# Decode attention of a hybrid layer: scores of both paged branches first, outputs afterwards

## The chip, the cores and the metric

The kernel runs on one core of a Trainium2 chip. The metric is the device time of one execution in microseconds (us), taken as the median of several runs. Besides, one execution is profiled, which gives the span of the core and a trace of every engine: PE (TensorE matmuls), PEld (its weight loads), DVE (VectorE), ACT (ScalarE), POOL (GpSimd) and SP (which here only issues transfers).

## What is computed

One inference step of a one-layer decoder, for a prompt of 1024 tokens and for 8 sampling sequences with one new token each:

```
p = rmsnorm(x, norm_g) @ w_in            # 1032 tokens x 2840 columns
q, cmp_kv, slc_kv, win_kv, gate logits, za, u, zp = split(p)
o_attn  = gate0*compressed(q) + gate1*selected(q) + gate2*window(q)   # 8 query heads, 2 KV heads, dim 64
o_pool  = causal means of u over 2/4/8/16 tokens, minus u, times pool_w and pool_scale
y = rmsnorm(x + concat(o_attn*silu(za), o_pool*silu(zp)) @ w_out, final_g)
```

For the 8 sampling sequences ("decode") each branch has a past of 256 tokens: the selected branch reads two pages of 128 rows per sequence from `cache_slc_kv` through a page table, the window branch reads 256 rows from `cache_win_kv`, and the compressed branch uses 15 blocks that an earlier stage of the kernel has computed. With so few blocks all of the past is selected, so the selected branch is plain attention over 257 keys (256 old ones and the new one), and so is the window branch.

## The kernel before, in words

The work stands in this order in the code: projection columns in token-major form (keys, values, gates), the compression of blocks together with the projection of the queries (`feat_unit`, lines 404 to 406), `decode()`, the pooling group, then the attention of the prompt in 32 units (`stage1` scores and softmax, `stage2` transposition and output), and between the steps of those units the filler work (the `za` gates with lines 979 to 981, the output projection with line 1053).

A scheduler orders the instructions of each engine ahead of time. It goes by a priority, mostly the place in the code, by estimated durations and by free buffers. `decode()` is emitted with a raised priority, as are the steps of the attention units. Thus in the machine code the decode instructions are strewn between the `feat_unit` matmuls of the pooling group (columns U and ZP, four groups `g`), which come after it in the code. Each engine then runs its own list strictly in order, and waits where an operand or a buffer isn't ready.

Names that matter below:

- `kvx` (4 buffers of 128 x 512 f32): a page of the selected branch, or 256 rows of the window of one sequence, keys and values together. It is fetched by an indirect transfer (line 640) or a plain one (line 644), both issued from POOL's queue.
- `dkt` (line 646): transposed keys in a PSUM bank of the ring `S` (3 banks). `kxh` and `kxl` (lines 656 and 657): their high and low part, one buffer each for four sequences.
- `vx` (8 buffers): the values split in a high part (ACT, line 651) and a low part (POOL, line 652). All eight sequences of a branch are held until the output matmuls of that branch (`dO`, line 684) have read them.
- `qx` and `px`: block-diagonal queries and probabilities, zeroed on POOL (lines 555 and 557). `pd`: the scores of a branch, and then its probabilities. `od`, `oq`: the sum of the outputs.
- PSUM rings: `S` with 3 banks (decode, and later the scores of the prompt), `tp` with 3 banks (`ps_t`: transpositions, and in the pooling group `ut`, line 810, and `yp`, line 849), `O` and `pj` with one bank each.
- The memory of `decode()`'s pool `dp` is given to the pool `at` of the prompt's attention (`qt`, `Ps`, `Pw`) when `decode()` is closed, each buffer as its last reader in `dp` is done. `stage1` of the first unit stands in the code within group 3 of the pooling part.
- `load_tile` (lines 393 and 143/144) fetches the weights of a `feat_unit` through SP and splits them on ACT and DVE.

`decode()` goes through the compressed branch first (lines 608 to 620), and then through the two other branches one after the other: scores, softmax, output.

Of the kernel before, what the change touches and what calls it, by code (L numbers as in the profile page):

```python
# [7 lines left out]
F32 = mybir.dt.float32  # L8
F32R = mybir.dt.float32r
I32 = mybir.dt.int32  # L10
BF16 = mybir.dt.bfloat16
AF = mybir.ActivationFunctionType
# [6 lines left out]
NB = 8  # L19
# [17 lines left out]
def r32(ap):  # L37
    return ap.bitcast(F32)
# [3 lines left out]
def hybrid_step_kernel(ctx, tc, xp, xs, ccmp, cslc, cwin, spool, ptab, norm_g, w_in, cmp_pe, cmp_w1,  # L42
                       cmp_w2, pool_w, pool_scale, w_out, final_g,
                       y_p, y_s, ncmp_p, nslc_p, nwin_p, npool_p, ncmp_s, nslc_s, nwin_s, npool_s):
    nc = tc.nc
# [11 lines left out]
    def ps_s(name="S"):  # L57
        return psum.tile([128, 512], F32, name=name, tag="S", bufs=3)

    def ps_t(name="tp"):  # L60
        return psum.tile([128, 512], F32, name=name, tag="tp", bufs=3)
# [22 lines left out]
    ident = pers.tile([128, 128], F32, name="ident")  # L84
# [254 lines left out]
    for br in range(2):  # L339
# [7 lines left out]
        for t in range(9):  # L347
            p, n = tok_unit(hi, lo, cn, t)
            if t < 8:
                f = kvf_tile(t)  # L350
# [11 lines left out]
                if t % 4 == 3:  # L362
                    c0 = (KS, KW)[br] + (t - 3) * 128
# [4 lines left out]
            else:  # L368
                f = p
# [76 lines left out]
    p = ps_t("pe_ps")  # L446
# [9 lines left out]
    Kcs = keep.tile([128, 128], F32, name="Kcs")  # L456
    Vcs = keep.tile([128, 128], F32, name="Vcs")
    zh = cp.tile([128, 8, NCOL + 4], F32R, name="zh")
    zl = cp.tile([128, 8, NCOL + 4], F32R, name="zl")
    for kind in range(2):  # L460
# [8 lines left out]
        for grp in range(3):  # L469
            tiles = pair_tiles(grp)  # L470
            for par in range(2):
                p = ps_t("z_ps")
                for m in range(4):
                    c0 = par * 256 + kind * 128
# [8 lines left out]
        for j in range(2):  # L483
            hi, lo = load_tile(dap(cmp_w1, (kind * 2 + j) * 16 * 64 * 128,
                                   [[128, 128], [16384, 8], [1, 128]]), cp)
            for s in range(8):
                mv = zh[:, s, j:j + NCOL + 2]
                first, last = j == 0 and s == 0, j == 1 and s == 7
# [3 lines left out]
                                 start=False, stop=last)  # L492
# [7 lines left out]
        if kind == 0:  # L500
            p = ps_t("kc_ps")
# [8 lines left out]
        else:  # L510
            p = ps_t("vc_ps")
            for kv in range(2):
                nc.tensor.matmul(p[:64, kv * 64:(kv + 1) * 64], H[:, kv * 192:kv * 192 + 64], w2v,
                                 start=True, stop=True)
# [4 lines left out]
            p = ps_t("vcs_ps")  # L519
            for kv in range(2):  # L520
                nc.tensor.matmul(p[:, kv * 64:(kv + 1) * 64], H[:, kv * 192 + 64:kv * 192 + 192], w2v,
                                 start=True, stop=True)
# [5 lines left out]
    for pt in range(4):  # L528
        hi, lo = load_tile(w_cols(C_Q + pt * 128))
        for c in range(3):  # L530
            p, t0, n = feat_unit(hi, lo, c)
# [16 lines left out]
    def decode():  # L548

        dp = des.enter_context(tc.tile_pool(name="dp", bufs=1, reuse_waits="tile"))  # L550

        qs = dp.tile([128, NB, 8], F32, name="qs")
# [1 line left out]
        nc.vector.memset(qs, 0.0)  # L554
        nc.gpsimd.memset(r32(qx), 0.0)
        px = dp.tile([128, 2, NB, 2, 64], F32R, name="px")
        nc.gpsimd.memset(r32(px), 0.0)

        def diag(ap):

# [10 lines left out]
        Kcs = dp.tile([128, 128], F32, name="Kcs")  # L571
# [26 lines left out]
        Pd = [Pd[0], Pd[1], Pd[0]]  # L598

        def dsoft(br, src, n):  # L600
            mx, nm, sm, rc = (st[:, br, k:k + 1] for k in range(4))
            nc.vector.tensor_reduce(mx, src, axis=AX.X, op=OP.max)
            nc.vector.tensor_scalar(nm, mx, -1.0, None, op0=OP.mult)
            nc.scalar.activation(Pd[br][:, :n], src, AF.Exp, bias=nm, accum_out=sm)
            nc.vector.reciprocal(rc, sm)
            nc.vector.tensor_scalar(Pd[br][:, :n], Pd[br][:, :n], rc, g64[:, br:br + 1], op0=OP.mult, op1=OP.mult)

        p = ps_s("dsc")
        nc.tensor.matmul(p[:64, :128], qs.rearrange("p b h -> p (b h)"), Kcs, start=True, stop=True)
        scs = Pd[0][:, :128]  # L610
        nc.vector.tensor_add(scs, p[:64, :128], cmask.rearrange("p b c -> p (b c)"))
        dsoft(0, scs, 128)
        p = ps_s("dpt")
        nc.tensor.transpose(p[:, :64], Pd[0][:, :128], ident[:64, :64])
        PcT = dp.tile([128, 64], F32, name="PcT")
        nc.vector.tensor_copy(PcT, p[:, :64])
        od = dp.tile([64, 128], F32, name="od")
        p = ps_s("dO0")
        nc.tensor.matmul(p[:64, :128], PcT, Vcs, start=True, stop=True)
        nc.vector.tensor_copy(od, p[:64, :128])  # L620
        for br in range(2):
            vx = []
            kn = dp.tile([128, NB], F32, name="kn", bufs=2)
            p = ps_s("dkn")
            nc.tensor.transpose(p[:, :NB], knew[br][:, :128], ident[:NB, :NB])
            nc.vector.tensor_copy(kn, p[:, :NB])
            sp = ps_s("dS")
            for b in range(0, NB, 2):
                if b % 4 == 0:
                    KXh = dp.tile([128, 4, 258], F32R, name="kxh")  # L630
                    KXl = dp.tile([128, 4, 258], F32R, name="kxl")
                    nc.vector.memset(r32(KXh[:, :, 257]), 0.0)
                    nc.vector.memset(r32(KXl[:, :, 257]), 0.0)
                    nc.vector.tensor_copy(KXh[:, :, 256], kn[:, b:b + 4])
                    nc.vector.tensor_sub(KXl[:, :, 256], kn[:, b:b + 4], r32(KXh[:, :, 256]))
                p = ps_s("dkt")
                for bb in range(2):
                    f = dp.tile([128, 512], F32, name="kvx", bufs=4)
                    if br == 0:
                        nc.gpsimd.indirect_dma_start(out=f, out_offset=None, in_=cslc,  # L640
                                                     in_offset=bass.IndirectOffsetOnAxis(
                                                         ap=idx[:, b + bb:b + bb + 1], axis=0))
                    else:
                        nc.gpsimd.dma_start(f, cwin[b + bb].rearrange("(p two) c -> p (two c)", two=2))
                    for par in range(2):
                        nc.tensor.transpose(p[:, (bb * 2 + par) * 128:(bb * 2 + par + 1) * 128],
                                            f[:, par * 256:par * 256 + 128], ident)

                    v = dp.tile([128, 2, 2, 128], F32R, name="vx", bufs=8)
                    fv = f.rearrange("p (two f c) -> p two f c", two=2, f=2)[:, :, 1]  # L650
                    nc.scalar.activation(v[:, :, 0], fv, AF.Copy)
                    nc.gpsimd.tensor_sub(v[:, :, 1], fv, r32(v[:, :, 0]))
                    vx.append(v)
                src = p.rearrange("p (b k) -> p b k", b=2)
                sl = (slice(None), slice(b % 4, b % 4 + 2), slice(0, 256))
                nc.scalar.activation(KXh[sl], src, AF.Copy)
                nc.vector.tensor_sub(KXl[sl], src, r32(KXh[sl]))
                for bb in range(b, b + 2):
                    w = qx[:, bb].rearrange("p f c -> p (f c)")
                    nc.tensor.matmul(sp[:, :258], w, KXh[:, bb % 4], start=bb == 0, stop=False)  # L660
                    nc.tensor.matmul(sp[:, :258], w, KXl[:, bb % 4], start=False, stop=bb == NB - 1)
            ss = Pd[br + 1]
            nc.scalar.activation(ss[:, :257], sp[64:, :257], AF.Copy)
            nc.vector.tensor_add(ss[:, :257], sp[:64, :257], ss[:, :257])
            dsoft(br + 1, ss[:, :257], 257)
            P_ = Pd[br + 1]
            dd = dp.tile([64, NB], F32, name="dd", bufs=2)
            nc.vector.tensor_scalar(dd, bmask, P_[:, 256:257], None, op0=OP.mult)
            p = ps_s("dptr")
            for par in range(2):  # L670
                nc.tensor.transpose(p[:, par * 64:(par + 1) * 64], P_[:, par * 128:(par + 1) * 128],
                                    ident[:64, :64])
            nc.tensor.transpose(p[:NB, 128:192], dd, ident[:64, :64])
            for par in range(2):
                src = p[:, par * 64:(par + 1) * 64].rearrange("p (b h) -> p b h", b=NB)
                ph, pl = (diag(px[:, par, 0, part, :]) for part in range(2))
                nc.scalar.activation(ph, src, AF.Copy)
                nc.vector.tensor_sub(pl, src, r32(ph))
            E_ = dp.tile([NB, 64], F32, name="dE", bufs=2)
            nc.vector.tensor_copy(E_, p[:NB, 128:192])  # L680
            p = ps_s("dO")
            for b in range(NB):
                for par in range(2):
                    nc.tensor.matmul(p[:, :256], px[:, par, b].rearrange("p f c -> p (f c)"), vx[b][:, par].rearrange("p f c -> p (f c)"),
                                     start=b == 0 and par == 0, stop=b == NB - 1 and par == 1)
            oq = dp.tile([64, 128], F32, name="oq")
            nc.scalar.activation(oq, p[64:, :128], AF.Copy)
            nc.vector.tensor_add(od, od, p[:64, :128])
            nc.vector.tensor_add(oq, oq, p[:64, 128:256])
            nc.vector.tensor_add(od, od, oq)  # L690
            p = ps_s("dOn")
            nc.tensor.matmul(p[:64, :128], E_, knew[br][:, 128:256], start=True, stop=True)
            nc.vector.tensor_add(od, od, p[:64, :128])
        p = ps_s("dOt")
        nc.tensor.transpose(p[:, :64], od, ident[:64, :64])
        odv = p[:, :64].rearrange("p (b h) -> p h b", h=8)
# [585 lines left out]
```

## Time and profile before

| | us |
|---|---|
| median of 3 runs | 638.68 (638.59 to 640.15) |
| the profiled execution, its own time | 638.69 |
| its span | 637.0 |
| PE busy in the span | 622.3 (98%) |
| DVE busy | 423.4 (66%) |
| ACT busy | 367.3 (58%) |
| POOL busy | 270.7 (43%) |

The busy time of an engine is the union of its instructions; matmuls overlap each other, and their ends are modelled. The time of an execution is the span and 1.7 us around it. Stretches are given in us from the span's start: the decode work lies between about 186 and 284, within the pooling group's matmuls, and the prompt's attention after it.

### The profile page before, as it was taken

The page shows a single profiled execution, that of the slowest core. Times are in us where ns is not written, and L with a number is a line of the kernel's source. Part 1 is how long each engine was busy: PE and PEld are TensorE (multiplying, and loading weights), DVE is VectorE, ACT ScalarE, POOL GpSimd, SP SyncE. Part 2 cuts the span into 40 slices and gives each one's busy share as a digit, 9 for nine tenths or more (in the row PEclk, how much of TensorE's full clock was granted, in tenths as well). Part 3 has the DMA queues.
Part 4 walks back from the last instruction along what each step waited for, and adds up shares of the span by engine and source line. Part 5 has one row for each costly group of instructions (what it writes and reads, how often), then busy time and mean ns, then how long its engine had stood idle before and what let it go on. Part 6 is the DMA issues. An engine that isn't in the chain of part 4 may idle for free.

```text
span 637.0 us, 12211 instructions
## 1 busy us (share of the span) xinstructions
PE 622.3 (98%) x4160; PEld 578.5 (91%) x4160; DVE 423.4 (66%) x1253; ACT 367.3 (58%) x947; POOL 270.7 (43%) x412
## 2 busy tenths in 40 slices
PE   8999999999999999999999999999999999999995
PEld 5999999999999899999899899789999988898895
DVE  6754234637364647466887999778978787877653
ACT  5654233526223333217887988777877777776652
POOL 6144004314035615005556767645554556444510
PEclk9999999999999999999999999999999999999999
DMA  8436106956224433333313357313113030101101
GB/s 281 152 90 157 34 1 201 314 196 181 74 79 133 138 102 95 92 110 101 100 35 99 100 182 214 107 30 101 37 50 100 18 100 16 67 19 67 51 2 66
DMA packets 63742, 65.13 MB, mean 102 GB/s; under 512 B 4488, under 2 KB 55120, under 8 KB 63640
## 3 DMA queue, kind: packets, MB, share of 16 engines
q1 hardware_dynamic: 53631, 44.55, 23.4%
q0 software_dynamic: 4000, 12.76, 6.2%
q10 hardware_dynamic: 6048, 7.05, 3.2%
q8 instruction: 33, 0.54, 0.4%
q14 instruction: 30, 0.24, 0.1%
HBM read 50.98 MB, written 15.68 MB: 105 GB/s over the span
## 4 chain that ended last, share of the span: by engine, by line
PE 93%; DVE 2%; ACT 1%; issue 1%; DMA 1%; POOL 1%; DVEq 0%; POOLq 0%; ACTq 0%
PE pj L1053 14%; PE S L777 10%; PE tp L902 9%; PE pa L404 7%; PE pa L406 7%; PE pa L405 7%; PE O L920 5%; PE O L919 5%; PE pa L277 4%; PE pa L275 3%; PE pa L276 3%; PE pj L979 2%; PE pj L980 2%; PE pj L981 2%; PE xtp_ps L230 1%; PE pj L1057 1%
## 5 line engine op out<-in xcount | busy, mean ns | idle before, releaser
L908 DVE TENSOR_TENSOR pl<-tp,ph 128x512 fp32r<-128x512 f32 (+1 forms) x136 | 89.9, 670 | 22.7 <-ACT ph L907 22.0
L777 PE MATMUL S<-KT,qt 128*128 128x320 f32 (+10 forms) x400 | 98.2, 346 | 3.0 <-DVE sm L736 3.0
L907 ACT ACTIVATE ph<-tp 128x512 fp32r<-128x512 f32 (+1 forms) x136 | 78.0, 580 | 38.3 <-PE tp L902 28.7
L404 PE MATMUL pa<-x,ws_hi 128*128 128x384 f32 (+1 forms) x288 | 93.7, 325 | 0.0
L406 PE MATMUL pa<-x,ws_lo 128*128 128x384 f32 (+1 forms) x288 | 92.9, 323 | 0.0
L405 PE MATMUL pa<-x,ws_hi 128*128 128x384 f32 (+1 forms) x288 | 92.7, 322 | 0.0
L1053 PE MATMUL pj<-wo,mh 128*128 128x512 f32 (+1 forms) x272 | 84.1, 387 | 0.0
L920 PE MATMUL O<-pl,V 128*128 128x256 f32 x264 | 75.7, 305 | 0.2
L919 PE MATMUL O<-ph,V 128*128 128x256 f32 x264 | 74.0, 296 | 0.0
L777 PEld LDWEIGHTS S<-KT,qt 128*128 128x128 f32 x400 | 63.7, 189 | 9.0 <-DVE sm L736 3.0
L796 POOL TENSOR_SCALAR Ps<-Ps,sm,gates 128x64 f32<-128x64 f32 (+5 forms) x88 | 62.9, 722 | 19.9 <-DVE sm L792 7.3
L789 ACT ACTIVATE Ps<-Ps,sm 128x64 f32<-128x64 f32 (+4 forms) x96 | 60.2, 628 | 16.4 <-DVE sm L736 14.8
L404 PEld LDWEIGHTS pa<-x,ws_hi 128*128 128x128 f32 x288 | 54.2, 188 | 0.5
L405 PEld LDWEIGHTS pa<-x,ws_hi 128*128 128x128 f32 x288 | 54.2, 188 | 0.4 <-issue 0.3
L406 PEld LDWEIGHTS pa<-x,ws_lo 128*128 128x128 f32 x288 | 54.2, 188 | 0.2
L277 PE MATMUL pa<-w_hi,x 128*128 128x256 f32 (+1 forms) x184 | 52.9, 288 | 1.2 <-DVE x L236 1.2
L275 PE MATMUL pa<-w_hi,x 128*128 128x256 f32 (+1 forms) x184 | 53.6, 292 | 0.0
L1053 PEld LDWEIGHTS pj<-wo,mh 128*128 128x128 f32 x272 | 47.2, 188 | 6.1 <-ACT mh L1205 0.3
L920 PEld LDWEIGHTS O<-pl,V 128*128 128x128 f32 x264 | 49.8, 189 | 3.1 <-DVE pl L908 0.6
L276 PE MATMUL pa<-w_lo,x 128*128 128x256 f32 (+1 forms) x184 | 52.4, 285 | 0.0
L1053 PE MATMUL pj<-wo,ml 128*128 128x512 f32 (+1 forms) x136 | 52.1, 383 | 0.0
L919 PEld LDWEIGHTS O<-ph,V 128*128 128x128 f32 x264 | 49.9, 189 | 1.8
(302 smaller groups left out, 1556.1 us busy)
## 6 DMA issues: line engine op xcount, KB each, us to landing
ws_raw<-in_w_in SPq DMA_DIRECT2D x32, 256.0 KB, 3.1
qt<-q_d SPq DMA_DIRECT2D x64, 128.0 KB, 2.9
x_t<-in_x_prompt SPq DMA_DIRECT2D x8, 512.0 KB
wo_raw<-in_w_out SPq DMA_DIRECT2D x8, 512.0 KB, 4.3
r<-in_x_prompt SPq DMA_DIRECT2D x8, 512.0 KB, 3.1
out<-r SPq DMA_DIRECT2D x7, 512.0 KB, 3.1
q_d<-qhl ACTq DMA_DIRECT2D x8, 384.0 KB, 4.0
out<-kvf ACTq DMA_DIRECT2D x5, 512.0 KB, 3.1
```

The costliest lines, as they stand in the source:

```text
L275: nc.tensor.matmul(p[:n, :cn], xh[c][:, k, ts_], hi[:, k, :cn], start=k == 0, stop=False)
L276: nc.tensor.matmul(p[:n, :cn], xh[c][:, k, ts_], lo[:, k, :cn], start=False, stop=False)
L277: nc.tensor.matmul(p[:n, :cn], xl[c][:, k, ts_], hi[:, k, :cn], start=False, stop=k == 7)
L404: nc.tensor.matmul(p[:, :n], hi[:, k, :], xh[c][:, k, :], start=k == 0, stop=False)
L405: nc.tensor.matmul(p[:, :n], hi[:, k, :], xl[c][:, k, :], start=False, stop=False)
L406: nc.tensor.matmul(p[:, :n], lo[:, k, :], xh[c][:, k, :], start=False, stop=k == 7)
L777: nc.tensor.matmul(S[:, :ln], qt[:, f, h, :], KT[:, kv, k0 + a:k0 + a + ln], start=f == 0, stop=f == 1)
L907: nc.scalar.activation(ph[:, :m], tp[:, :m], AF.Copy)
L908: nc.vector.tensor_sub(pl[:, :m], tp[:, :m], r32(ph[:, :m]))
L919: nc.tensor.matmul(O[:, :256], vv, ph[:, a * 256:(a + 1) * 256], start=False, stop=False)
L920: nc.tensor.matmul(O[:, :256], vv, pl[:, a * 256:(a + 1) * 256], start=False, stop=last)
L1053: nc.tensor.matmul(p, a[:, k % 4, :], w, start=first and kk == 0, stop=last and kk == 2)
```

## The change

The three branches are put in another order. `dscores(br)` holds the score part of a paged branch, `dout(br, ...)` its output part. The order in the code becomes: scores of the selected branch; zeros for `px`; scores of the window branch; output of the selected branch; the window's values; the whole compressed branch; output of the window branch. In the window branch the keys of two sequences share one `kvx` buffer and come in transfers of their own, 16 transfers of half the size in all in place of 8, and the values come in the other half of these. The transposed keys `dkt` go to the `tp` ring. The compressed branch keeps its probabilities in a buffer of the name `oq`. The first output that is added to `od` is now that of the selected branch.

```
-        nc.gpsimd.memset(r32(px), 0.0)
...
-        p = ps_s("dsc")
-        nc.tensor.matmul(p[:64, :128], qs.rearrange("p b h -> p (b h)"), Kcs, start=True, stop=True)
-        scs = Pd[0][:, :128]
-        nc.vector.tensor_add(scs, p[:64, :128], cmask.rearrange("p b c -> p (b c)"))
-        dsoft(0, scs, 128)
...
-        nc.vector.tensor_copy(od, p[:64, :128])
-        for br in range(2):
+        def split_v(v, fv):
+            nc.scalar.activation(v[:, :, 0], fv, AF.Copy)
+            nc.gpsimd.tensor_sub(v[:, :, 1], fv, r32(v[:, :, 0]))
+
+        def dscores(br):
...
-                p = ps_s("dkt")
+                p = ps_t("dkt")
+                if br == 1:
+                    f = dp.tile([128, 512], F32, name="kvx", bufs=4)
+                    for bb in range(2):
+                        nc.gpsimd.dma_start(f[:, bb * 256:(bb + 1) * 256].rearrange("p (two c) -> p two c", two=2),
+                                            cwin[b + bb].rearrange("(p two) c -> p two c", two=2)[:, :, :128])
                 for bb in range(2):
-                    f = dp.tile([128, 512], F32, name="kvx", bufs=4)
                     if br == 0:
+                        f = dp.tile([128, 512], F32, name="kvx", bufs=4)
                         nc.gpsimd.indirect_dma_start(out=f, out_offset=None, in_=cslc,
...
-                    else:
-                        nc.gpsimd.dma_start(f, cwin[b + bb].rearrange("(p two) c -> p (two c)", two=2))
...
-                    v = dp.tile([128, 2, 2, 128], F32R, name="vx", bufs=8)
-                    fv = f.rearrange("p (two f c) -> p two f c", two=2, f=2)[:, :, 1]
-                    nc.scalar.activation(v[:, :, 0], fv, AF.Copy)
-                    nc.gpsimd.tensor_sub(v[:, :, 1], fv, r32(v[:, :, 0]))
-                    vx.append(v)
+                    if br == 0:
+                        v = dp.tile([128, 2, 2, 128], F32R, name="vx", bufs=8)
+                        split_v(v, f.rearrange("p (two f c) -> p two f c", two=2, f=2)[:, :, 1])
+                        vx.append(v)
...
+        def win_values():
+            vx = []
+            for b in range(0, NB, 2):
+                f = dp.tile([128, 512], F32, name="kvx", bufs=4)
+                for bb in range(2):
+                    fv = f[:, bb * 256:(bb + 1) * 256].rearrange("p (two c) -> p two c", two=2)
+                    nc.gpsimd.dma_start(fv, cwin[b + bb].rearrange("(p two) c -> p two c", two=2)[:, :, 128:])
+                    v = dp.tile([128, 2, 2, 128], F32R, name="vx", bufs=8)
+                    split_v(v, fv)
+                    vx.append(v)
+            return vx
+
+        def dout(br, vx, first=False):
...
-            nc.vector.tensor_add(od, od, p[:64, :128])
+            if first:
+                nc.vector.tensor_copy(od, p[:64, :128])
+            else:
+                nc.vector.tensor_add(od, od, p[:64, :128])
...
+        vx0 = dscores(0)
+        nc.gpsimd.memset(r32(px), 0.0)
+        dscores(1)
+        dout(0, vx0, True)
+        vx1 = win_values()
+
+        p = ps_s("dsc")
+        nc.tensor.matmul(p[:64, :128], qs.rearrange("p b h -> p (b h)"), Kcs, start=True, stop=True)
+        scs = Pd[0] = dp.tile([64, 128], F32, name="oq")
+        nc.vector.tensor_add(scs, p[:64, :128], cmask.rearrange("p b c -> p (b c)"))
+        dsoft(0, scs, 128)
+        p = ps_s("dpt")
+        nc.tensor.transpose(p[:, :64], Pd[0][:, :128], ident[:64, :64])
+        PcT = dp.tile([128, 64], F32, name="PcT")
+        nc.vector.tensor_copy(PcT, p[:, :64])
+        p = ps_s("dO0")
+        nc.tensor.matmul(p[:64, :128], PcT, Vcs, start=True, stop=True)
+        nc.vector.tensor_add(od, od, p[:64, :128])
+        dout(1, vx1)
```

## Rows read from the trace of the kernel before

**Rows 1.** The page's busy times: engine, busy us (share of the span) and instructions.

```profile
PE 622.3 (98%) x4160; PEld 578.5 (91%) x4160; DVE 423.4 (66%) x1253; ACT 367.3 (58%) x947; POOL 270.7 (43%) x412
```

**Rows 2.** Busy time of the engines by stretch, then clock, DMA share and GB/s.

```profile
0.00:20.00 20.00, 16.60 (x83) 11.39 (x84) 13.91 (x19) 10.52 (x19) 11.35 (x25) 1.00 0.78 264
...
150.00:180.00 30.00, 30.00 (x194) 29.97 (x193) 13.92 (x28) 12.05 (x25) 6.28 (x8) 1.00 0.42 123
...
180.00:280.00 100.00, 99.19 (x639) 93.88 (x638) 57.71 (x150) 30.64 (x75) 36.73 (x51) 1.00 0.38 111
...
290.00:340.00 50.00, 49.02 (x339) 46.08 (x340) 37.63 (x174) 40.97 (x152) 30.20 (x63) 1.00 0.25 69
...
340.00:380.00 40.00, 39.46 (x279) 37.80 (x278) 35.79 (x115) 34.04 (x96) 29.24 (x40) 1.00 0.41 133
380.00:420.00 40.00, 38.31 (x260) 33.28 (x259) 33.71 (x115) 31.23 (x84) 24.13 (x38) 1.00 0.48 146
420.00:460.00 40.00, 40.00 (x265) 36.10 (x264) 35.02 (x115) 30.04 (x77) 20.37 (x32) 1.00 0.20 61
...
630.00:637.00 7.00, 0.41 (x4) 0.20 (x2) 2.34 (x8) 1.53 (x5) 0.00 (x0) 0.80 0.19 75
```

**Rows 3.** What PE waited for over the span: us in total, times, longest.

```profile
PE S L777 <- DVE sm L736: 3.0, 6, 1.0
...
PE dkt L646 <- DMA kvx<-in_cache_slc_kv,idx: 0.8, 2, 0.6
PE tp L902 <- DVE pc L898: 0.4, 1, 0.4
```

**Rows 4.** PE in order of time: start, length, line, operation, [idle before and releaser].

```profile
206.73 0.66 PE L646 MATMUL dkt<-ident,kvx 128*128 128x128 f32 x4
...
218.58 0.41 PE L646 MATMUL dkt<-ident,kvx 128*128 128x128 f32 x2 [0.56 <-DMA kvx<-in_cache_slc_kv,idx]
...
225.42 0.28 PE L661 MATMUL dS<-kxl,qx 128*128 128x258 f32 x1
...
242.72 0.60 PE L646 MATMUL dkt<-ident,kvx 128*128 128x128 f32 x4
...
281.81 0.27 PE L695 MATMUL dOt<-ident,od 64*128 64x64 f32 x1
...
287.39 0.81 PE L777 MATMUL S<-KT,qt 128*128 128x192 f32 x6
288.61 1.95 PE L777 MATMUL S<-KT,qt 128*128 128x128 f32 x12 [0.40 <-DVE sm L736]
```

**Rows 5.** POOL in order of time, the decode part.

```profile
187.31 1.83 POOL L557 MEMSET px<- 128x2048 f32 x1
...
189.53 0.98 POOL L640 DMA_INDIRECT kvx<-in_cache_slc_kv,idx  x1 [0.16 <-issue]
...
207.45 1.87 POOL L640 DMA_INDIRECT kvx<-in_cache_slc_kv,idx  x1 [5.76 <-PE dkt L646]
...
237.57 4.91 POOL L652 TENSOR_TENSOR vx<-kvx,vx 128x256 fp32r<-128x256 f32 x4 [11.14 <-ACT vx L651]
243.66 1.11 POOL L644 DMA_DIRECT2D kvx<-in_cache_win_kv  x2 [1.18 <-PE dkt L646]
```

**Rows 6.** Groups of instructions by line: busy us, mean ns, idle before.

```profile
L640 POOL DMA_INDIRECT kvx<-in_cache_slc_kv,idx x8 | 9.6, 1194 | 7.6 <-PE dkt L646 5.8 <-issue 1.8
L656 ACT ACTIVATE kxh<-dkt 128x512 fp32r<-128x512 f32 x8 | 4.6, 592 | 2.7 <-PE dkt L646 2.7
L657 DVE TENSOR_TENSOR kxl<-dkt,kxh 128x512 fp32r<-128x512 f32 x8 | 5.4, 684 | 3.4 <-ACT kxh L656 3.4
L644 POOL DMA_DIRECT2D kvx<-in_cache_win_kv x8 | 4.5, 566 | 1.2 <-PE dkt L646 1.2
```

**Rows 7.** Transfers by line: queue, count, KB each, median us from issue to landing.

```profile
qt<-q_d SPq DMA_DIRECT2D x64, 128.0 KB, 2.9
...
kvx<-in_cache_win_kv POOLq DMA_DIRECT2D x8, 256.0 KB, 3.2
...
kvx<-in_cache_slc_kv,idx POOLq DMA_INDIRECT x8, 3.6
```

**Rows 8.** SP's queue in order of time, the end of the decode part.

```profile
267.98 0.97 SPq L393 DMA_DIRECT2D ws_raw<-in_w_in  x2
272.03 0.37 SPq L860 DMA_DIRECT2D out<-utok  x1
272.45 0.56 SPq L861 DMA_DIRECT2D out<-utok  x1
273.12 1.29 SPq L732 DMA_DIRECT2D qt<-q_d  x2
```

**Rows 9.** ACT in order of time: the split of the weights fetched at 267.98.

```profile
281.20 1.15 ACT L143 ACTIVATE ws_hi<-ws_raw 128x512 fp32r<-128x512 f32 x2 [2.36 <-PE pa L405]
```

More of the change, by code (lines that the diff above doesn't have):

```diff
@@ L606, in dsoft @@
             nc.vector.tensor_scalar(Pd[br][:, :n], Pd[br][:, :n], rc, g64[:, br:br + 1], op0=OP.mult, op1=OP.mult)
-        p = ps_s("dsc")
-        nc.tensor.matmul(p[:64, :128], qs.rearrange("p b h -> p (b h)"), Kcs, start=True, stop=True)
-        scs = Pd[0][:, :128]
-        nc.vector.tensor_add(scs, p[:64, :128], cmask.rearrange("p b c -> p (b c)"))
-        dsoft(0, scs, 128)
[L613 to L616, printed above, removed]
         od = dp.tile([64, 128], F32, name="od")
-        p = ps_s("dO0")
-        nc.tensor.matmul(p[:64, :128], PcT, Vcs, start=True, stop=True)
-        nc.vector.tensor_copy(od, p[:64, :128])
-        for br in range(2):
+        def split_v(v, fv):
+            nc.scalar.activation(v[:, :, 0], fv, AF.Copy)
+            nc.gpsimd.tensor_sub(v[:, :, 1], fv, r32(v[:, :, 0]))
+        def dscores(br):
             vx = []
@@ L642, in decode @@
                                                          ap=idx[:, b + bb:b + bb + 1], axis=0))
-                    else:
-                        nc.gpsimd.dma_start(f, cwin[b + bb].rearrange("(p two) c -> p (two c)", two=2))
                     for par in range(2):
+                        c0 = par * 256 if br == 0 else bb * 256 + par * 128
                         nc.tensor.transpose(p[:, (bb * 2 + par) * 128:(bb * 2 + par + 1) * 128],
-                                            f[:, par * 256:par * 256 + 128], ident)
-                    v = dp.tile([128, 2, 2, 128], F32R, name="vx", bufs=8)
-                    fv = f.rearrange("p (two f c) -> p two f c", two=2, f=2)[:, :, 1]
-                    nc.scalar.activation(v[:, :, 0], fv, AF.Copy)
-                    nc.gpsimd.tensor_sub(v[:, :, 1], fv, r32(v[:, :, 0]))
-                    vx.append(v)
+                                            f[:, c0:c0 + 128], ident)
+                    if br == 0:
+                        v = dp.tile([128, 2, 2, 128], F32R, name="vx", bufs=8)
+                        split_v(v, f.rearrange("p (two f c) -> p two f c", two=2, f=2)[:, :, 1])
+                        vx.append(v)
                 src = p.rearrange("p (b k) -> p b k", b=2)
@@ L665, in decode @@
             dsoft(br + 1, ss[:, :257], 257)
+            return vx
[9 more added lines that the diff above has]
+                    vx.append(v)
+            return vx
+        def dout(br, vx, first=False):
             P_ = Pd[br + 1]
```

## The prediction

> **What bounds the kernel now.** The page's busy times come first [rows 1]: PE is busy for 622.3 of 637.0 us, the next engine for 423.4. So a change of the order can only gain what PE stands still for, or what it works badly; work hidden beside PE is worth nothing in itself. The table by stretch [rows 2] says where that is. In 150 to 180, before decode, PE is busy all the time and loads weights for 29.97 of 30.00 us. In 180 to 280, which holds nearly all of decode, it stands for 0.81 us of 100, while DVE, ACT and POOL have 42, 69 and 63 us to spare. From 290 to 420 it stands for 0.98 + 0.54 + 1.69 us, and from 340 on DVE has only some 10 of 80 us to spare; after 420 the next standing shown is that at the very end. The list of PE's waits [rows 3] names the causes: 0.8 us in two waits for the second four pages of the selected branch, 3.0 us in six waits for DVE to empty a score bank of the prompt's attention, and 0.4 us for DVE at line 898. The sum, 4.2 us, is nearly all that an order can take out as waiting: of PE's 14.7 us of standing (637.0 - 622.3), 3.4 lie in the first 20 us and 6.6 in the last 7, where the change has nothing.
>
> PE's timeline [rows 4] gives the decode chain: first key transposition at 206.73, last score matmul of the selected branch at 225.42, first transposition of the window at 242.72, the end of decode with `dOt` at 281.81, first prompt scores at 287.39. The `feat_unit` matmuls fill PE throughout. Decode takes long but is on nobody's path, until the prompt's attention wants its memory.
>
> **Part by part.** *PE's work.* Nothing is removed or added: 32 transpositions, 32 score and 32 output matmuls and the compressed branch's few stay as they are, each in the same shape. 0 us.
>
> *DVE and ACT.* The copy into `od` and an addition change places; all splits stay. 0 us, and beyond that hidden by the idle time in 180 to 280 [rows 2].
>
> *POOL.* The zeros of `px` (1.83 us) stood ahead of the first page transfer (187.31 against 189.53 [rows 5]); they now follow the selected scores, so that all first pages leave up to 1.8 us earlier. `px` was first written long after, and POOL has 63 us free there: 0 us at its new place. Without that cover it would be 1.8 us.
>
> *Transfers.* The window's 8 issues of 566 ns become 16 [rows 6], 4.5 us more on POOL; at the price of an indirect issue (1194 ns) they would be 16 x 1.19 - 4.5 = 14.5 us more. Both fit in POOL's 63 free us: 0. What stands behind them in POOL's queue are the low halves of `vx` and the `bb` products of the pooling group; the latter's results are wanted only by stores and by filler work. The halves have runs of 512 bytes in place of 2 KB. The nearest row with such a size and such runs is the `qt` load (128 KB, runs of 128 f32): 2.9 us from issue to landing, against 3.2 for the 256 KB of today [rows 7]. I take 2.9, no loss for a half; the values' halves are not wanted until after two softmaxes. Here the Trainium skill speaks against the change: its page "DMA: Bandwidth & Descriptors", "Rules for kernel authors", wants many small transfers made one, and its section on the anatomy of a DMA gives each a fixed part of about 2.0 us. By the page, eight more transfers would cost an estimated 16 us if nothing hid them, against nothing by the row, since the landings overlap beside PE.
>
> *Where decode's waits go.* Three things held the chain. First, the compressed branch: pages were landed well before 206.73 (the first four were issued from 189.53 on, and land in 3.6 us [rows 5, 7]), yet the first transposition follows the compressed branch and its S banks. Now it can start near 195 to 200, some 8 us earlier, and the second four pages, whose issue waited 5.76 us for that transposition [rows 5], follow. Second, the window's keys shared buffers with its values, which had to wait for `vx`, thus for the selected output: POOL's four splits at 237.57 came after 11.14 us of idling, and only then could the next two window rows be fetched, at 243.66. Now window transpositions can follow the selected scores directly: from 225.42 to 242.72 were 17 us, of which I give back most. Together decode should end some 20 to 30 us earlier, at about 255 instead of 282. Its own latest part is then the window's values: `vx` free after the selected output, then 8 splits.
>
> *What that is worth.* PE's list is full of `feat_unit` matmuls up to 283 in either case, so an earlier end of decode gives PE nothing there. It gives memory: `qt`, `Ps` and `Pw` lie where decode's buffers lay, and with these free the first unit's scores (287.39 [rows 4]) can be strewn into the pooling group, where DVE and ACT are idle. That removes the wait of 0.40 us right behind them; I take 0.4. The other waits lie between 290 and 420 [rows 2], where the same units meet the same filler in the same priority; I take none. The two page waits (0.56 [rows 4], and 0.8 in sum [rows 3]) come from PE's list being written with estimated landings; the same four indirect loads and eight new window loads remain, so the wait can vanish or be repeated. Bounds: 0 and, at this wait for each of the eight pairs of pages, 8 x 0.4 = 3.2 us. I take half of the present, 0.4: nearer to zero than to the top, since the second four pages leave sooner and no plain transfer was ever waited for.
>
> *The `tp` ring.* `dkt` leaves `S` for the three banks that `yp` and `ut` use. A `yp` matmul may now wait for the two readers of a `dkt` bank, 0.59 + 0.68 us [rows 6]: at worst 1.3 us in each of four groups, 5 us. With three banks, and readers on engines that are half idle, I take 0, and keep some of it for the range.
>
> Sum: 638.7 - 0.4 - 0.4 = 637.9 us. The profiled execution (638.69) equals the median of the runs, so nothing is to be converted.
>
> **Rivals.** *Faster* by more than 1.9 us (0.3%, what a measurement of this kernel can tell from no change). The prompt's attention gets ahead by a unit or more in 255 to 283, and DVE no longer holds PE up before 420. Then all of 4.2 us goes [rows 3]: 634.5; half of it is about the bound, 636.8. PE's busy row may even hide more: in 180 to 280 weights were loaded for 93.88 of 100 us, against 29.97 of 30 before [rows 2], so at most 6.1 us are lost to mixing decode into the stream, and getting back a third of them, 2 us, would do. For it speaks that exactly this stretch has idle DVE; against it, that short decode matmuls remain and are as many. The Trainium skill ("Trainium Kernel Development and Optimization", "Performance Expectations") calls matmul busy time a bad metric and weight-load busy time a good one; by that rule the faster case would have those 6.1 us to take, against 0.81 by PE's row, and its chance is a little higher for it.
>
> *Slower* by more than 1.9 us: PE's list stands still for pages. Place: the window key transpositions, moved right behind the selected scores, in a list that is in order, with every `feat_unit` matmul queued behind. Price: 0.4 us for each of eight pairs, +3.2, less the 0.8 of today: 641.1; it decides from 2.7 us of waiting in all. A page reached right at its issue would cost PE up to 3.2 to 3.6 us at once [rows 7]. For it: the only waits of this stretch are of this kind. Against: plain window transfers caused none so far.
>
> *No effect on the end of decode*, because output buffers still chain the branches: then 638.7, within the "same".
>
> *SP's queue blocked.* `qt` loads, drawn forward, could stand in SP's queue ahead of `ws_raw` and wait there for decode's buffers. Weights issued at 267.98 were split at 281.20 only [rows 8, 9], so a block of up to some 12 us costs nothing; above that, every us is one. I count it in the slower case.
>
> **Chances.** Change within 0.3%, my forecast: 0.54. Faster: 0.27. Slower: 0.19. The range reaches from 635.0, where the faster case has nearly all its waits back, to 641.0, the page waits of the slower case: 8 in 10. The likeliest case's own range is 636.8 to 640.6.
>
> **What the profile would show.** Right: first `dkt` before 202, window transpositions before 235, `dOt` before 265, first prompt scores before 283, and PE's busy time within 1 us of 622.3, since its work is the same. The page waits would be a row of PE's waits with `kvx` as releaser: under 1 us by the forecast, over 2.7 by the slower case. The DVE waits of 3.0 us would stay by the forecast and fall below 1.5 in the faster case. Wrong would be: a new releaser of PE (`tp` banks, `ws_lo`) with more than 2 us, or a PE busy time that moves by more than 2 us.

## The result, and the profile after

The changed kernel takes 647.1 us (median of 4 runs, 646.39 to 647.9) against 638.66: 1.0124 of the time before, interval 1.0111 to 1.0137. It is slower by 8.4 us; I had forecast 637.9, with 641.0 as the upper end. The profiled execution took 647.76 us with a span of 646.1, 9.1 more than before.

The page's busy times, as in [rows 1]:

```profile
PE 626.3 (97%) x4160; PEld 582.1 (90%) x4160; DVE 422.5 (65%) x1253; ACT 367.1 (57%) x947; POOL 277.8 (43%) x420
```

The table by stretch, columns as in [rows 2]:

```profile
180.00:280.00 100.00, 97.61 (x616) 90.89 (x616) 56.56 (x169) 33.49 (x92) 44.19 (x65) 0.98 0.42 119
210.00:240.00 30.00, 27.61 (x161) 23.38 (x160) 24.36 (x65) 11.79 (x31) 17.47 (x25) 0.94 0.33 98
290.00:340.00 50.00, 47.97 (x338) 46.09 (x337) 39.60 (x172) 40.01 (x143) 27.60 (x56) 1.00 0.27 75
340.00:380.00 40.00, 39.73 (x270) 37.84 (x270) 33.47 (x115) 32.06 (x90) 24.23 (x37) 1.00 0.21 67
380.00:420.00 40.00, 37.12 (x263) 33.49 (x262) 34.11 (x116) 32.80 (x86) 28.89 (x40) 1.00 0.55 179
...
632.00:640.00 8.00, 5.51 (x29) 4.88 (x27) 3.91 (x11) 1.92 (x6) 0.45 (x1) 0.79 0.00 0
```

What PE waited for over the span, as in [rows 3]:

```profile
PE S L812 <- DVE sm L771: 2.6, 2, 1.5
PE pj L1088 <- ACT mh L1240: 2.0, 1, 2.0
PE O L948 <- DVE pc L933: 1.3, 1, 1.3
...
PE dS L658 <- DVE kxl L654: 0.8, 1, 0.8
...
PE pj L1014 <- DVE zt L1000: 0.7, 1, 0.7
PE pa L404 <- DVE sz L412: 0.6, 1, 0.6
PE yp L884 <- PE dO L696: 0.6, 1, 0.6
PE yp L884 <- DVE ws L867: 0.4, 1, 0.4
```

PE in order of time, as in [rows 4]. Behind the decode part all lines of the code stand 35 further down than before, so that L884 is the old L849 (`yp`) and L1088 the old L1053 (the output projection):

```profile
193.85 0.38 PE L645 MATMUL dkt<-ident,kvx 128*128 128x128 f32 x2
...
209.58 0.38 PE L645 MATMUL dkt<-ident,kvx 128*128 128x128 f32 x2
...
217.15 0.27 PE L845 MATMUL ut<-ident,u 128*15 128x128 f32 x1
...
217.47 0.38 PE L645 MATMUL dkt<-ident,kvx 128*128 128x128 f32 x2
...
219.31 0.39 PE L658 MATMUL dS<-kxl,qx 128*128 128x258 f32 x1 [0.82 <-DVE kxl L654]
...
221.29 3.45 PE L884 MATMUL yp<-ws,pw 128*128 128x384 f32 x6 [0.57 <-PE dO L696]
...
228.46 0.39 PE L404 MATMUL pa<-x,ws_hi 128*128 128x264 f32 x1 [0.61 <-DVE sz L412]
...
258.12 0.27 PE L730 MATMUL dOt<-ident,od 64*128 64x64 f32 x1
...
266.65 0.69 PE L812 MATMUL S<-KT,qt 128*128 128x192 f32 x5
...
631.92 0.28 PE L955 MATMUL O<-pl,V 128*128 128x256 f32 x1
634.15 0.81 PE L1088 MATMUL pj<-wo,mh 128*128 128x512 f32 x2 [1.96 <-ACT mh L1240]
```

The first `ut` and the first `yp` in the kernel before:

```profile
183.47 0.27 PE L810 MATMUL ut<-ident,u 128*15 128x128 f32 x1
...
195.11 1.90 PE L849 MATMUL yp<-ws,pw 128*128 128x384 f32 x6
```

Decode is earlier, as planned: its last transposition stands at 258.12 in place of 281.81 [rows 4], the prompt's first scores at 266.65 in place of 287.39. The time is lost in three other places. Set against [rows 2]:

- **180 to 280.** PE stands for 2.39 us in place of 0.81, and the granted clock has a mean of 0.98 in place of 1.00, which I estimate at some 2 us of 100. Together 3.6. Nearly all of it lies in 210 to 240. The first `yp`, at 195.11 before, stands at 221.29, right behind decode's last keys, and its six matmuls take 3.45 us, where six took 1.90 before. Ahead of it the first `ut`, from which `us`, then `ws` and then `yp` are computed, has moved from 183.47 to 217.15.
- **290 to 420.** PE stands for 2.03 + 0.27 + 2.88 = 5.18 us in place of 3.21: 2.0 more. The waits there are those for `pc` (1.3 us), `zt` (0.7) and `sm` (2.6 in two).
- **The end.** Between the last `O` and the output projection PE stands for 1.96 us, and behind it the clock is low: 0.79 over 632 to 640, some 1.7 us. Together 3.6. Before, PE did not stand there at all.

The sum, 9.2, is close to the span's 9.1. Two of the places lie where decode is long over.

### The profile page after: what moved, and what is told of

Read it like the earlier page. It is cut to its first block, busy times and chain, and to the rows that moved or that the text cites. A ratio compares the mean times of both kernels' runs of the same rounds, so it can differ in the third digit from the quotient of the medians.

```text
span 646.1 us, 12231 instructions
## 1 busy us (share of the span) xinstructions
PE 626.3 (97%) x4160; PEld 582.1 (90%) x4160; DVE 422.5 (65%) x1253; ACT 367.1 (57%) x947; POOL 277.8 (43%) x420
## 4 chain that ended last, share of the span: by engine, by line
PE 86%; DVE 6%; issue 4%; ACT 2%; DMA 1%; POOL 1%; POOLq 0%; DVEq 0%; ACTq 0%
PE pj L1088 13%; PE S L812 9%; PE tp L937 8%; PE pa L404 7%; PE pa L406 7%; PE pa L405 7%; PE O L955 4%; PE O L954 4%; PE pa L277 3%; PE pa L275 3%; PE pa L276 3%; PE pj L1014 2%; PE pj L1015 2%; PE pj L1016 2%; PE xtp_ps L230 1%
## 5 line engine op out<-in xcount | busy, mean ns | idle before, releaser
L1088 PE MATMUL pj<-wo,mh 128*128 128x512 f32 (+1 forms) x272 | 84.7, 391 | 2.0 <-ACT mh L1240 2.0
L831 POOL TENSOR_SCALAR Ps<-Ps,sm,gates 128x64 f32<-128x64 f32 (+5 forms) x88 | 64.3, 738 | 24.4 <-DVE sm L827 22.3
L1088 PEld LDWEIGHTS pj<-wo,mh 128*128 128x128 f32 x272 | 48.9, 194 | 8.6 <-ACT mh L1240 2.2
L1088 PE MATMUL pj<-wo,ml 128*128 128x512 f32 (+1 forms) x136 | 52.6, 388 | 0.0
L824 ACT ACTIVATE Pw<-Pw,sm 128x640 f32<-128x640 f32 (+4 forms) x64 | 44.3, 692 | 14.3 <-DVE sm L771 11.0
```

The source lines that it names most:

```text
L824: e = nc.scalar.activation(regs[br], regs[br], AF.Exp, scale=-1.0, bias=sm[:, hh, 0, br:br + 1], accum_out=sm[:, hh, 1, br:br + 1])
L1088: nc.tensor.matmul(p, a[:, k % 4, :], w, start=first and kk == 0, stop=last and kk == 2)
```

## The experiments

Each is told with its edit against the changed kernel ("after") or the kernel before; none leaves out work. In the three sets the kernel before ran at 638.73, 638.79 and 638.70 us.

**Keys back in `S`.** The changed kernel with one word undone.

```diff
-                p = ps_t("dkt")
+                p = ps_s("dkt")
```

> The changed kernel with the transposed keys back in the S ring; order and transfers as changed. Theory 'ring': in tp the keys take all three banks ahead of yp, the first yp comes at 221 instead of 195, and the DVE work of the pooling group is pushed into the same 15 us as decode's; then here yp comes before 200 again, PE stands for less than 1 us in 205 to 245, the half clock there is gone, and the time is 640 to 643 (the loss at the end may stay). Rival 'order': it is the scores of both branches right behind one another that crowd DVE; then PE still stands for over 1.5 us in 205 to 245 and the time is 645 to 647.

Measured: 641.97 us, 1.0043 of before (1.0026 to 1.0059), so 5.1 us of the 8.4 are gone. The first `yp` is back at 194.87, and decode's stretch is whole:

```profile
205.00:245.00 40.00, 39.78 (x263) 37.77 (x262) 24.04 (x65) 16.92 (x42) 22.14 (x32) 1.00 0.43 123
```

In that stretch the banks were the cause, not the order of decode.

**The `tp` banks alone.** The kernel before, with `ps_t("dkt")` and nothing else of the change.

> The kernel before with one edit: the transposed keys in the tp ring. Theory 'ring': the first yp moves behind the selected branch, PE stands for 1.5 us or more in 205 to 245, and the time is 642 to 645. Rival 'order': the ring alone does nothing or helps a little, 637 to 639.5.

Measured: 659.69 us, 1.0327 (1.0308 to 1.0345). The sign was expected, the size not: 21 us, more than the whole change loses. PE in order of time shows how:

```profile
214.64 0.34 PE L406 MATMUL pa<-x,ws_lo 128*128 128x384 f32 x1
...
220.47 0.41 PE L671 MATMUL dptr<-ident,pd 64*128 64x64 f32 x2 [4.11 <-DVE pd L606]
...
230.90 0.27 PE L810 MATMUL ut<-ident,u 128*15 128x128 f32 x1
...
232.23 0.38 PE L646 MATMUL dkt<-ident,kvx 128*128 128x128 f32 x2
...
234.56 2.90 PE L849 MATMUL yp<-ws,pw 128*128 128x384 f32 x4 [0.88 <-PE dS L660]
...
242.91 0.59 PE L404 MATMUL pa<-x,ws_hi 128*128 128x264 f32 x1 [4.18 <-DVE sz L412]
```

Decode runs at priority 1000, so its next pair of pages takes each `tp` bank that comes free. The first to be held is `ut`: it stands at 230.90, behind all but the last pair of keys, and `yp`, which is computed from it, follows at 234.56. (Which tile holds a bank is not in the trace; it is read from the order of PE's list.) Behind `yp` wait `bb` and, as `sz` has a single buffer (L840), the next group's `pa` matmuls. From 214.64 to 242.91 the trace has not one `pa` matmul: the filler is gone, and PE stands for each softmax and split of decode (4.11 us for `pd`). The stretch, and the page's busy times:

```profile
205.00:245.00 40.00, 28.27 (x141) 23.76 (x140) 21.02 (x65) 11.63 (x29) 13.60 (x20) 0.78 0.27 82
```

```profile
PE 629.5 (96%) x4160; PEld 585.7 (89%) x4160; DVE 422.3 (64%) x1253; ACT 366.8 (56%) x947; POOL 268.2 (41%) x412
```

In it PE stands for 11.7 us, and the granted clock has a mean of 0.78. Over the whole span of 657.6 us PE stands 13.4 us longer than before (28.1 against 14.7) and is busy 7.2 us longer for the same matmuls (629.5 against 622.3): 20.6 us, the growth of the span. In the changed kernel the keys of both branches go through `tp` without the softmax and the outputs between them, and the last are transposed at 217.47 in place of 232.23; the new order makes the same fault cheaper.

**Own transfers alone.** The changed kernel with the order and the banks of before; only the window's keys and values in their own transfers are left.

```diff
-        vx0 = dscores(0)
         nc.gpsimd.memset(r32(px), 0.0)
-        dscores(1)
-        dout(0, vx0, True)
-        vx1 = win_values()
...
+        dout(0, dscores(0))
+        dscores(1)
+        dout(1, win_values())
...
-                p = ps_t("dkt")
+                p = ps_s("dkt")
```

> Order and ring as before, only the window's keys and values come in transfers of their own. All theories that hold the transfers for harmless: 637.5 to 640, no wait of PE for kvx of the window. Rival 'transfers': the sixteen issues crowd POOL and the low halves of the values come late; over 641.

Measured: 638.46 us, 0.9995 (0.9986 to 1.0005). The transfers cost nothing, as the prediction had it. The Trainium skill's page "DMA: Bandwidth & Descriptors" (section on the anatomy of one DMA) gives a transfer a fixed part of about 2.0 us, an estimated 16 us for eight more if nothing hid them; this run shows none of it.

**The order of the end.** In the changed kernel, the last output tile's first nine matmuls are kept behind the last `O`, where the trace of before has them.

```diff
-            if j and k == 0:
-                after(ins[n0], last_mm)
+            if k == 0:
+                after(ins[n0], last_mm if j else O_["lastO"])
```

> The changed kernel, and the first nine matmuls of the last output tile are kept behind the last matmul of the last attention unit. Theory 'end': in the changed kernel nothing is left on PE while the last unit's result goes through ACT, DVE, POOL, ACT (1.96 us of standing, then some 3.3 us at half clock), so that here some 3 us come back: 643 to 645. Rival: the end only shows a delay that comes from before; then no more than 0.5 us comes back, 646 to 648.

Measured: 643.65 us, 1.0065 (1.0049 to 1.0082): 3.4 us less than the changed kernel, as the wait and the low clock there had added up to. PE in order of time around the last `O` of this run:

```profile
630.42 0.28 PE L955 MATMUL O<-pl,V 128*128 128x256 f32 x1
630.54 0.62 PE L1088 MATMUL pj<-wo,mh 128*128 128x512 f32 x2
```

And in the kernel before, the last `O`, and the first and the tenth matmul behind it:

```profile
624.36 0.28 PE L920 MATMUL O<-pl,V 128*128 128x256 f32 x1
624.48 0.62 PE L1053 MATMUL pj<-wo,mh 128*128 128x512 f32 x2
...
626.60 0.74 PE L1053 MATMUL pj<-wo,mh 128*128 128x512 f32 x2
```

The chain from the last `O` over `ol`, `ou` and `za` to `mh` is the same in all kernels. Before, 36 output matmuls followed the last `O`, and the first nine (2.1 us) covered it; in the changed kernel only 27 followed, the nine others having been strewn in ahead of it.

**The same edit in the kernel before**, as a control.

> The kernel before with only the order of the end written out (nine matmuls of the last output tile behind the last `O`), as a control for that edit. Both theories: the order is already that, so 638.7 us, between 638.2 and 639.2. A gain of over 1 us here would mean that the edit is worth something by itself, and that its 3.4 us in the changed kernel aren't due to the changed end.

Measured: 638.85 us, 1.0003 (0.9993 to 1.0012). So the edit is worth nothing where the order was already that.

**Both repairs.** The changed kernel with `dkt` in `S` and the written-out end.

> The changed kernel with two edits together: the key transpositions `dkt` back in the `S` banks, and the last output tile's first nine matmuls kept behind the last `O`. Theory `ring and end` (the ring costs 5.1 us, the end 3.4 us, and nothing else of the change costs anything): 638.5 us, between 637.5 and 639.5, and no PE wait on `mh` or `zt` at the end. Theory `order` (the later outputs shift the prompt's attention, which then loses time by waits on `sm` that the filler no longer covers): 640.5 to 642 us, with such a wait of 2 us or more still there. Theory `the new order is worth something once the ring is repaired`: under 637.5 us.

Measured: 640.59 us, 1.0027 (1.0016 to 1.0037). That is the range of the theory `order`, not 638.5: the two repairs give 6.5 together, 5.1 and 3.4 alone, since the keys in `S` already bring back part of the end (its wait was 0.8 us in that run), while the longest wait on `sm` grew from 1.5 us in the changed kernel to 3.6 with the keys in `S`. A wait of over 2 us on `sm` is there, as that theory had it. But the order of time around it, ACT, DVE and PE, names another cause (the traced execution took 642.39 us, the longest of the ten, so the median one may have lost less there):

```profile
402.11 1.15 ACT L1036 ACTIVATE wo<-wo_raw 128x512 fp32r<-128x512 f32 x2 [4.24 <-DMA wo_raw<-in_w_out]
402.77 0.69 DVE L1037 TENSOR_TENSOR wo<-wo_raw,wo 128x512 fp32r<-128x512 f32 x1 [3.99 <-ACT wo L1036]
...
403.99 0.87 PE L812 MATMUL S<-KT,qt 128*128 128x320 f32 x2 [4.42 <-DVE sm L771]
```

PE waits for DVE, DVE for ACT, and ACT for an output weight that had not landed. SP's queue in the same run, and in the kernel before:

```profile
378.91 0.81 SPq L1228 DMA_DIRECT2D out<-in_cache_win_kv  x1
...
392.55 2.49 SPq L1033 DMA_DIRECT2D wo_raw<-in_w_out  x2
```

```profile
372.40 0.81 SPq L1193 DMA_DIRECT2D out<-in_cache_win_kv  x1
...
384.39 2.49 SPq L998 DMA_DIRECT2D wo_raw<-in_w_out  x2
```

A copy of 2 MB (the window cache, unit 14) stands ahead of the load. Before, the load was issued 8.2 us earlier, and ACT has no wait on it there (its splits begin at 396.10). In the changed kernel itself the copy stands at 387.74, and ACT's two waits for such loads (0.94 us at 373.36, 1.58 at 393.46) are for loads issued ahead of it; no load behind the copy is waited for there.

**The copy later.** The run above with the copy, and the small one of the pool state next to it, in unit 22.

```diff
-        if x == 14:
+        if x == 22:
```

> The changed kernel with `dkt` in `S` and the written-out end (that run gave 640.59), and the 2 MB copy of the window cache with the pool state issued in unit 22 instead of unit 14. Theory `copy` (the last 1.8 us are the 4.4 us wait near 404 us, where the `wo_raw` load stands in line with that copy): the wait on `wo_raw` falls under 1.5 us and the time is 637.5 to 639. Theory `order` (the reordering costs it in another way, or SP is late anyway): 640 to 641.5 us.

Measured: 637.57 us (637.3 to 638.83, 11 runs), 0.9986 of before (0.9977 to 0.9995): 3.0 us less than without the edit, and 1.1 us under the kernel before, by little but with an interval that leaves out 1. The load is issued at 386.53, of ACT's 4.9 us of waiting for `wo_raw` 0.4 are left, and PE's waits on `sm` fall from 6.0 to 2.3 us. The stretch 380 to 420 without the edit, and with it:

```profile
380.00:420.00 40.00, 35.30 (x241) 32.65 (x241) 31.38 (x104) 30.03 (x80) 25.57 (x37) 0.96 0.62 190
```

```profile
380.00:420.00 40.00, 39.12 (x268) 34.52 (x267) 33.51 (x110) 32.18 (x86) 26.41 (x38) 1.00 0.45 129
```

**The same in the kernel before.**

> The kernel before with only that copy issued in unit 22. In it no engine waited for `wo_raw` at that place, so by the theory `copy` the time stays: 638.3 to 639.2 us. If the copy hurts whatever stands around it: under 638.0 us.

Measured: 638.96 us, 1.0000 (0.9990 to 1.0009). The copy costs nothing in that order. So the reordering itself, with its transfers, is worth 638.96 - 637.57 = 1.4 us, once the banks, the end and this queue are put right around it.

**`yp` in other banks, three runs.** To tell "`yp` is held back" from "keys go badly in `tp`", `yp` and `ut` were moved to the `O` and `pj` banks: in the changed kernel with the written-out end, in the kernel before with keys in `tp`, and in the kernel before as it is.

```diff
-        p = ps_t("ut")
+        p = ps_any("ut")
...
-            p = ps_t("yp")
+            p = ps_any("yp")
```

> The changed kernel with `dkt` left in the `tp` banks, but `yp` and `ut` of the pooling groups moved to the `O` and `pj` banks, and the last nine matmuls kept behind the last `O`. Theory `held back` (the `tp` banks hurt only because the pooling's `yp` stands behind decoding's keys in them, so its bank is what matters): first `yp` between 190 and 200 us, no PE wait over 0.5 us between 205 and 245 us, and 638 to 641 us. Theory `tp banks as such` (the keys themselves go badly in `tp`, or the `S` banks miss them): 643 us or more, like the run with the end alone (643.65).

> The kernel before with `dkt` in the `tp` banks (which alone gave 659.7 us), and `yp` and `ut` in the `O` and `pj` banks. Theory `held back`: most of the 21 us goes away; 639 to 648 us, with the first `yp` near 195 us. What the end costs in another order (up to 6 us) may stay, seen as a wait on `mh` after 630 us. Theory `tp banks as such`: 655 us or more, with the waits on `sz` and `pd` of some 4 us between 215 and 245 us still there.

> The kernel before with only `yp` and `ut` of the pooling moved to the `O` and `pj` banks; the keys `dkt` stay in `S`. It is the control for the run that had both moves (652.38). Theory `held back` (keys in `tp` cost nothing once `yp` isn't in the same banks; what was left there, 13.6 us, is the price of `yp` in the two banks of the feature matmuls): 650 to 654 us, with PE waits on `us`, `u` and `bb` of 1 us and more between 180 and 260 us. Theory `tp banks as such`: 638 to 643 us, so that the 13.6 us would be due to the keys in `tp`.

Measured: 652.48 (1.0216), 652.38 (1.0208) and 668.02 us (1.0457). All three missed the numbers of `held back`; the first lies in the range of its rival (643 or more), the other two in neither range. The first `yp` did come early (193.98, 194.38 and 193.60), and the waits of some 4 us for `sz` and `pd` were gone, but the two new banks are also those of the `pa` matmuls, and PE now waits there. Its waits in the third run:

```profile
PE yp L849 <- DVE bb L852: 5.5, 3, 3.0
...
PE ut L810 <- ACT u L808: 1.6, 2, 1.4
```

So the move has a price of its own, 29.3 us in the kernel before, and the first run can't tell the theories apart. The last two can: with `yp` out of the way, keys in `tp` are 15.6 us better than keys in `S` (652.38 against 668.02), where with `yp` in `tp` they were 21 us worse. So the 21 us come from sharing the banks with `yp` and `ut`, not from the keys being in `tp`. Why it is a gain of 15.6 and not nought was not followed up, and as both kernels are far slower than before, that keys in `tp` would cost nothing in a sound kernel is not shown.

## Why the prediction was wrong

**Right.** PE's work, DVE and ACT, `px`, and the transfers at nothing (landings of 2.9 us in the changed kernel; 3.2 us, and 638.46 in all, with them alone). Decode's chain: first `dkt` at 193.85 (before 202), the ninth of 16 pairs, the window's first, at 209.58 (before 235), `dOt` at 258.12 against "about 255", first scores at 266.65 (before 283). No wait for pages is left, so the slower case's own mechanism did not happen. And an earlier end of decode was worth little, 1.4 us.

**The step that failed: the `tp` ring**, "at worst 1.3 us in each of four groups, 5 us", taken as 0. It asked how long a reader of a `dkt` bank takes (0.59 + 0.68 us, [rows 6]). The question was who gets the bank next. With decode ahead in priority it is the next `dkt`, for nearly all of sixteen pairs of transpositions. The first `ut`, which the step names and gives no price, moved from 183.47 to 217.15, and `yp`, which needs it, from 195.11 to 221.29. Nor is `yp` filler that may come late: `bb`, the single `sz` and the next group's matmuls hang on it, which are all that covers decode. Undoing that one word gives 5.1 us back (net of the longer wait on `sm`), and doing it alone costs 21. The step's worst, 5 us, happens to be near the first and far from the second, because it was priced as the wrong thing.

**The end and the attention**, "the same units meet the same filler in the same priority; I take none". The priorities are the same, but what has been spent of the filler by then is not, nor is the place of a load in SP's queue. Nine matmuls of the last output tile moved ahead of the last `O` (3.4 us), and a weight load came to stand behind a 2 MB copy until it was too late (3.0 us, seen only with the other two repaired; the 2.0 us that the changed kernel lost between 290 and 420 were not taken apart). Neither place is near the change. I had seen the end only as 6.6 us "where the change has nothing" [rows 2]. A blocked queue of SP was among the rivals, but for `qt` ahead of `ws_raw`.

**The terms taken as gains.** The two page waits went, as in the better half of what I took (0.8 us). So did the wait of 0.40 us behind the first unit's scores: from 280 to 290 PE now stands for nothing, where it stood for 0.42. But the waits on `sm` as a whole only fell from 3.0 to 2.6 us, and those for `pc` and `zt` were added. All are small beside 8.4. With the three places put right the time is 637.57, near the forecast 637.9; of the 6.1 us of weight loads missing in 180 to 280 that the faster case counted on, that kernel has 0.8 back (94.70 against 93.88).

**The last test.** A busy time of PE that moves by more than 2 us was named as what would show the forecast wrong, and it did: up by 4.0 us for the same matmuls, nearly the 2.0 + 1.7 us of low clock. A single new releaser with more than 2 us was not there; the largest, `mh`, has 1.96, and the rest is strewn.

## What to carry to other kernels

A buffer ring that a high-priority stage shares with filler is priced by how long that stage goes on asking for it, not by how long it holds one buffer; what then hangs on the filler's next step through single buffers is the bill, here 5 to 21 us for one word. After any reorder, look at the places where cover was exactly enough, the last matmuls and the loads behind large copies, since a planner that spends filler at a pace moves them without being asked. Such losses hide a gain too: with three places put right, the reordering that had cost 8.4 us won 1.1.

## What the runs showed of the hardware

A stall can cost more than its length, when the clock falls with it. After the 4.11 and 0.72 us of standing in the run with the `tp` banks alone, the same score matmul (128x258) followed its predecessor by 0.21 to 0.22 us (227.95 to 229.03, at a granted clock of 0.50, which is 1.2 GHz) where it had been 0.12 (211.77 to 212.37, at 1.00, 2.4 GHz). In that run 13.4 us more of standing came with 7.2 us more of busy time for the same matmuls. At the end of the changed kernel 1.96 us of standing came with some 1.7 of low clock. Not every wait does it: those on `sm` in the kernel before, 1.0 us at the longest [rows 3], left the mean clock of 290 to 420 at 1.00 [rows 2].

One plain DVE addition on 64x128 took 3.83 us in the changed kernel, and 3.83 again with the written-out end, where its other execution took 0.28. It ran while POOL did six splits of values in a row, and both ended within 0.2 us of each other:

```profile
230.47 3.83 DVE L705 TENSOR_TENSOR od<-od,oq 64x128 f32<-64x128 f32 x1
```

```profile
229.94 4.20 POOL L612 TENSOR_TENSOR vx<-kvx,vx 128x256 fp32r<-128x256 f32 x6
```

That the one holds the other up is what this suggests, but with the keys in `S` the same addition took 0.35 us in the midst of eight such splits, so they are not enough to explain it, and the cause stays open:

```profile
238.74 0.35 DVE L705 TENSOR_TENSOR od<-od,oq 64x128 f32<-64x128 f32 x1
```

```profile
236.14 6.08 POOL L612 TENSOR_TENSOR vx<-kvx,vx 128x256 fp32r<-128x256 f32 x8 [7.33 <-ACT vx L611]
```
